# A two-layer encoder on one core: order of the first gate units of each feed-forward part pinned, and the last key projection moved by one block

## The chip, the cores and the metric

One Trainium2 chip, one core. The metric is the device time of one execution in microseconds. The engines are TensorE (PE, with its weight loads PEld), VectorE (DVE), ScalarE (ACT), GpSimd (POOL) and SyncE (SP), whose queue issues nearly all DMAs.

## The reference, cut

The input is x of 1 × 1024 × 1024 in float32. Layer 0 mixes with multi-head latent attention, layer 1 with differential attention; each layer is

```python
h = _layernorm(ALPHA * h + mix, ln_mix_g[i], ln_mix_b[i])
h = _layernorm(ALPHA * h + _swiglu(h, ffn_w_gu[i], ffn_w_down[i]), ln_ffn_g[i], ln_ffn_b[i])
```

with

```python
def _swiglu(x, w_gu, w_down):
    gate, up = jnp.split(x @ w_gu, 2, axis=-1)
    return (jax.nn.silu(gate) * up) @ w_down
```

The hidden width D_FF is 2816. In mixer B each of 8 heads has two softmax maps over 1024 keys in blocks of 128 queries (chunk-causal mask, ALiBi distances), and the output is map 0 minus lambda times map 1, times the values.

## The kernel before

**Precision.** Every large product is made of three matmuls in fp32r: a high part (a cast on ACT) and a low part (the source minus the high part, a subtract on DVE or POOL) of each operand, high × high, high × low, low × high. `split` (L501) makes the pair, and `op_unit` (L508) makes it for one unit of weights, 128 × 512, in one of a few shared buffers. So each block of weights goes DMA, cast on ACT, subtract on DVE or POOL, then PE.

**The feed-forward part** (`ffn`, L520) is a Strassen-like scheme of seven products on 2 × 2 blocks. A unit n (22 of them in a layer) is one block of w_gu, with four sub-blocks a11, a12, a21, a22; the products have the names "1", "2", "6", "7", "5", "4" and "3", 12 matmuls of 512 columns each. "1" and "2" use x itself, the others sums of blocks of x (t1, t2, t3, t4, b22), made by `raw_x` (L463) and cast by `part` (L706). `prepare` (L569) makes a product's operand: sums of sub-blocks on DVE (L579 a21 + a22, L581 a21 − a11, L583 a12 − a11, L587 a22 − a11), then `op_unit`. `consume` (L595) issues the matmuls (L547) and what reads the result. "6", "7" and "4" add into one PSUM bank, gb: after "6" DVE reads it (L629, into tmp), after "7" again (L633), and after "4" (L639). The next of the three can't begin before the read. "5" and "3" go to gc and are added by L631 and L635, "1" and "2" to ga.

**The early units.** For the first npre = 6 units "1" and "2" come first, while the last rows of the layer norm ahead are not there yet: `load_pre` (L559) loads half of unit n's block (tile gp, 2 buffers) and makes both operands, with the subtract on POOL for n = 0, 1 and on DVE from 2 on; `gates(n)` (L681) issues the products of units n and n + 1, and for n > 0 stores their results to DRAM (pg_dr), from which they are loaded again later. `load` (L553) loads a whole unit (tile gr, 1 MB).

**The layer norm** (L163) of a block of 128 rows: two means (nmu, L166, L167), squares on ACT (L170), the centred rows (L176), variance (ve, L178), a power on POOL (rs, L180), the result (L183). `raw_x` transposes it on PE (xTp), and DVE and ACT make the blocks of x (L482 to L486). In front of FFN1 the last such block, z_a, runs between the early units (`pending`).

**Mixer B.** `fill` slots say which projection is issued beside which block of attention. For head h, `proj_b` (L1369) makes queries (which = 0) and keys (which = 1), half by half: 24 matmuls, then casts (L1395) and subtracts (L1396) into the key tile bk. `score_b` (L1398) makes the scores of a block of 128 queries for both maps (L219; the maximum L222 on DVE, the exponential L227 on ACT), a reciprocal (L1411), and the difference of the maps (L1412 on POOL, L1413 on DVE); `turn_b` transposes it (pt, L148), `mix_b` multiplies it by the values. Three PSUM banks serve the scores.

**What sets the order.** The instructions are listed by a scheduler with high and low priorities from program order, so that an edit re-orders neighbours on all engines. `behind(i, j)` (L155) is a pin: instruction i may not stand ahead of j on their engine; it adds no semaphore.

## Time and profile before

| | |
|---|---|
| time, median of 3 runs | 2272.02 us (2271.24 to 2272.13) |
| the profiled execution | 2270.85 us |
| its span | 2269.1 us |
| PE busy | 2240.7 us |
| mean granted clock | 0.997 |
| FFN of layer 0 | about 440 to 1080 us |
| mixer B | about 1080 to 1545 us |
| FFN of layer 1 | about 1622 to 2269 us |

Busy times are of one profiled execution. A matmul record's start is when PE takes it; neighbours overlap, so the distance of two starts tells the rate, not the duration. A value in brackets behind a row is the idle time of that engine ahead of it, and what ended it. PEclk is the clock granted to TensorE as a share of the full one. Buffer numbers are left out of the trace's names, so gb, gr, op_g and tmp of all units read alike. The line numbers are those of the kernel before.

### The profile page before, as it was taken

The numbers are of one execution on the slowest core, as the hardware profiler recorded it, in microseconds if no ns is written. First come the engines' busy times: TensorE is split into PE (matmuls) and PEld (weight loads), VectorE is DVE, ScalarE is ACT, GpSimd is POOL, SyncE is SP. The second block draws the span as 40 slices with busy tenths as digits, with TensorE's granted clock in tenths as the row PEclk, the third lists the DMA queues.
The fourth block names the chain that finished last, engine by engine and source line by source line (L and its number), as shares of the span: only waits on it lengthen the run. The fifth ranks groups of instructions, "written<-read, shape, count | busy, mean of one in ns | idle before, by whom it ended". The sixth has DMA issues, their size and how long they took to land.

```text
span 2269.1 us, 31052 instructions
## 1 busy us (share of the span) xinstructions
PE 2240.7 (99%) x11410; PEld 1913.2 (84%) x11410; DVE 1547.0 (68%) x2894; ACT 1013.8 (45%) x2097; POOL 775.2 (34%) x626
## 2 busy tenths in 40 slices
PE   8999999999999999999999999999999999999998
PEld 8899998888888888888888898988778888888886
DVE  5676665686766667777576667576687656668778
ACT  4455564342333334445465656564432333334444
POOL 2232341114444440455432424221114444430561
PEclk9999999999999999999999999999999999999999
DMA  5010125434435338554310212053244223238443
GB/s 203 14 35 31 42 70 194 143 128 144 171 135 199 119 122 329 184 187 158 103 47 24 66 38 69 14 221 139 103 155 151 93 98 111 96 113 326 166 179 151
DMA packets 105545, 287.76 MB, mean 127 GB/s; under 512 B 7968, under 2 KB 30112, under 8 KB 94896
## 3 DMA queue, kind: packets, MB, share of 16 engines
q1 hardware_dynamic: 101552, 277.44, 34.4%
q0 software_dynamic: 3840, 8.33, 1.4%
q8 instruction: 90, 1.47, 0.3%
q14 instruction: 63, 0.52, 0.1%
HBM read 204.47 MB, written 77.07 MB: 124 GB/s over the span
## 4 chain that ended last, share of the span: by engine, by line
PE 94%; DVE 3%; DMA 1%; issue 1%; ACT 1%; POOL 0%; SPq 0%; DVEq 0%; POOLq 0%
PE gb L547 15%; PE ga L547 10%; PE gc L547 10%; PE dw L858 7%; PE dx L858 5%; PE s_a L219 4%; PE zp_a L417 3%; PE s_b L219 3%; PE dv L858 3%; PE dy L858 3%; PE bp L145 3%; PE bp L143 3%; PE bp L144 3%; PE o_a L262 2%; PE o_b L262 2%; PE hq L1107 1%
## 5 line engine op out<-in xcount | busy, mean ns | idle before, releaser
L503 ACT CAST op_g<-gr 128x512 fp32r<-128x512 f32 x240 | 146.7, 621 | 369.9 <-PE gb L547 183.1
L504 POOL TENSOR_TENSOR op_g<-gr,op_g 128x512 fp32r<-128x512 f32 x104 | 145.7, 1406 | 248.0 <-ACT op_g L503 139.6
L504 DVE TENSOR_TENSOR op_h<-rh,op_h 128x512 fp32r<-128x512 f32 x152 | 142.3, 962 | 49.4 <-ACT op_h L503 49.4
L547 PE MATMUL ga<-xh_m,op_g 128*128 128x512 f32 x512 | 168.2, 389 | 0.0
L858 PE MATMUL dw<-op_w_t,op_h 128*128 128x512 f32 x660 | 151.3, 390 | 0.0
L503 ACT CAST op_h<-rh 128x512 fp32r<-128x512 f32 x152 | 91.8, 619 | 126.7 <-PE dx L858 35.4
L858 PEld LDWEIGHTS dw<-op_w_t,op_h 128*128 128x128 f32 x660 | 123.5, 188 | 25.9 <-DVE op_h L504 0.4
L227 ACT ACTIVATE l_b<-l_b,mx_b 128x256 f32<-128x256 f32 (+7 forms) x128 | 99.4, 776 | 75.3 <-DVE mx_b L222 73.4
L504 POOL TENSOR_TENSOR op_w_b<-rw_b,op_w_b 128x512 fp32r<-128x512 f32 x44 | 64.3, 1484 | 175.5 <-ACT op_w_b L503 168.2
L858 PE MATMUL dx<-op_w_b,op_h 128*128 128x512 f32 x528 | 121.5, 390 | 1.0 <-DVE op_w_b L504 1.0
L1412 POOL TENSOR_SCALAR l_b<-l_b,rb,cst 128x128 f32<-128x128 f32 (+3 forms) x64 | 52.5, 821 | 203.8 <-DVE rb L1411 192.5
L504 DVE TENSOR_TENSOR op_g<-gr,op_g 128x512 fp32r<-128x512 f32 x136 | 110.6, 818 | 14.2 <-ACT op_g L503 14.0
L547 PE MATMUL gb<-t4h_f,op_g 128*128 128x512 f32 x352 | 115.8, 390 | 3.1 <-DVE tmp L633 3.1
L858 PEld LDWEIGHTS dx<-op_w_b,op_h 128*128 128x128 f32 x528 | 98.8, 188 | 23.0 <-DVE op_w_b L504 2.6
L547 PE MATMUL gb<-t2h_f,op_g 128*128 128x512 f32 x352 | 115.6, 390 | 0.4 <-DVE op_g L504 0.4
L547 PE MATMUL gc<-t1h_f,op_g 128*128 128x512 f32 x352 | 115.6, 389 | 0.0
L547 PE MATMUL gc<-b22h_f,op_g 128*128 128x512 f32 x352 | 115.3, 389 | 0.0
L547 PE MATMUL gb<-t3h_f,op_g 128*128 128x512 f32 x352 | 115.2, 389 | 0.0
L547 PEld LDWEIGHTS ga<-xh_m,op_g 128*128 128x128 f32 x512 | 96.1, 188 | 20.0
L504 POOL TENSOR_TENSOR op_g<-s,op_g 128x512 fp32r<-128x512 f32 x40 | 55.1, 1378 | 167.1 <-ACT op_g L503 158.8
L143 PE MATMUL bp<-xT_f,h_wb 128*128 128x512 f32 x256 | 101.6, 397 | 0.0
L144 PE MATMUL bp<-xT_f,h_wb 128*128 128x512 f32 x256 | 101.5, 397 | 0.0
(388 smaller groups left out, 6696.5 us busy)
## 6 DMA issues: line engine op xcount, KB each, us to landing
gr<-in_w_gu SPq DMA_DIRECT2D x44, 1024.0 KB, 6.9
rh<-h_dr SPq DMA_DIRECT2D x28, 1024.0 KB, 5.4
h_dr<-sh SPq DMA_DIRECT2D x22, 1024.0 KB, 5.1
h_dr<-hp SPq DMA_DIRECT2D x22, 768.0 KB, 4.1
tt<-in_w_dn SPq DMA_DIRECT2D x22, 512.0 KB, 7.3
rh<-h_dr SPq DMA_DIRECT2D x12, 768.0 KB, 4.4
wo_dr<-op_pwo SPq DMA_DIRECT2D x16, 512.0 KB, 3.5
z<-xs_dr SPq DMA_DIRECT2D x16, 512.0 KB, 11.9
```

The lines of the kernel that those rows point to most:

```text
L143: T.matmul(ps_out, lh, rh, start=(i == 0), stop=False)
L144: T.matmul(ps_out, lh, rl, start=False, stop=False)
L145: T.matmul(ps_out, ll, rh, start=False, stop=(i == n - 1))
L219: T.matmul(s[:, :w], lh, rh[:, ks], start=(j == 0), stop=(j == len(q_pass) - 1))
L227: ends["exp"] = A.activation(l[:, :n], l[:, :n], AF.Exp, bias=mx, scale=-1.0, accum_out=sm).ins
L262: T.matmul(po[:, c], a, b[:, j % 2, c], start=st, stop=sp_, skip_group_check=True)
L417: T.matmul(m, a[:, h, :], self.wo[h][w][:, c], start=(start and h == heads[0] and a is oh and w == 0), stop=(stop and h == heads[-1] and a ...
L503: turns["cast"] = A.copy(hi, src).ins
L504: return eng.tensor_tensor(lo, src, f32(hi), ALU.subtract).ins
L547: T.matmul(o, w[:, a, k * P:(k + 1) * P], x[b][:, k, :], start=(first and k == 0 and (a, b) == (0, 0)), stop=(k == 3 and a == 1), skip_gro ...
L858: T.matmul(o, h[:, a, c], w[:, b_], start=(first and (a, b_) == (0, 0)), stop=(last and a == 1), skip_group_check=True,).ins for a, b_ in ...
L1412: G.tensor_scalar(l1[:, :n], l1[:, :n], r[:, 1:2], nlam, ALU.mult, ALU.mult)
```

## The change

Three regions are touched: the start of the FFN in layer 0, its start in layer 1 (the same code), and the last head of mixer B. The number of matmuls, casts, subtracts and transfers is the same.

- `layer_norm` records its centred rows and its last result, `raw_x` its last operation, `consume` the copy of unit n's first product. In `load_pre` the subtracts of unit 2 are pinned behind the centred rows, those of units 3 to 5 behind the layer norm's result; the first cast of unit 3 is pinned behind the copy of the last first product issued.
- `load_pre(3)` is called after `gates(0)`.
- The first sum of units 0 and 1 (L579) is pinned behind raw_x's last operation.
- The products "6", "7", "4" of units 0 and 1 take turns in the program's order.
- The casts of b22 are pinned behind unit 4's last cast, those of t3 behind unit 5's first.
- In the last head of mixer B the last half of the key projection is issued in slot 4 rather than 5.

```diff
@@ layer_norm
         centred = V.scalar_tensor_tensor(y, z, nmu[:, 1:2], g, ALU.add, ALU.mult)
+        ends["centred"] = centred.ins
...
-            V.scalar_tensor_tensor(y[:, c], y[:, c], rs, b[:, c], ALU.mult, ALU.add)
+            ends["ln"] = V.scalar_tensor_tensor(y[:, c], y[:, c], rs, b[:, c], ALU.mult, ALU.add).ins
@@ raw_x
-            V.tensor_tensor(b21, b21, b12, ALU.add)
+            ends["x"] = V.tensor_tensor(b21, b21, b12, ALU.add).ins
@@ load_pre
                 ops[n, pr] = op_unit(t[:, i], eng, f"gp{layer}_{n}_{pr}")
+                early_cast[n, pr] = turns["cast"]
+                if eng is V:
+                    behind(turns["last"], ends["centred" if n == 2 else "ln"])
+                if n == 3 and pr == "1":
+                    behind(turns["cast"], ends["p1"])
@@ prepare
-                V.tensor_tensor(a21, a21, a22, ALU.add)
+                i = V.tensor_tensor(a21, a21, a22, ALU.add).ins
+                if n < 2:
+                    behind(i, ends["x"])
@@ consume
-                    A.copy(p1, acc[n, "a"])
+                    ends["p1"] = A.copy(p1, acc[n, "a"]).ins
@@ ffn
-        for n in range(4):
+        for n in range(3):
             load_pre(n, G if n < 2 else V)
         gates(0)
+        load_pre(3, V)
...
-        for n in range(NFF):
-            stream += [(n, pr) for pr in ("674" if n < 2 else "67543" if n < npre else "1627543")]
+        stream += [(n, pr) for pr in "674" for n in range(2)]
+        for n in range(2, NFF):
+            stream += [(n, pr) for pr in ("67543" if n < npre else "1627543")]
...
         load_pre(4, V)
+        cast = turns["cast"]
         for k in range(4):
             part("b22", k, r22, V)
+            behind(turns["cast"], cast)
         load_pre(5, V)
+        cast = early_cast[5, "1"]
...
             part("t3", k, r11, V)
+            behind(turns["cast"], cast)
@@ mixer B
-            for j, slot in enumerate((2, 3, 5, 6) if h < H - 1 else (1, 2, 3, 5)):
+            for j, slot in enumerate((2, 3, 5, 6) if h < H - 1 else (1, 2, 3, 4)):
```

In the rows that follow, the numbers behind a name tell buffers, and lines of the changed kernel are up to 14 higher than those of the kernel before for the same code.

On DVE in front of FFN1, in the layer norm of the last rows (nmu, z_a and ve belong to it, op_gp_2 to the early unit 2, xr_m to the blocks of x); before:

```order
L167 TENSOR_SCALAR nmu_a_1_16093<-sum_a_1_16036 128x1
L504 TENSOR_TENSOR op_gp_2_2_16160<-gp_2_16155,op_gp_2_2_16160 128x512
L504 TENSOR_TENSOR op_gp_2_1_16157<-gp_2_16155,op_gp_2_1_16157 128x512
L484 TENSOR_TENSOR xr_m_15516<-xr_m_15515,xTp_a_0_0_16106 128x4x128
L485 TENSOR_TENSOR xr_m_15514<-xr_m_15514,xTp_a_0_1_16111 128x4x128
L176 SCALAR_TENSOR_TENSOR z_a_0_15945<-z_a_0_15945,nmu_a_1_16093,gb_15518 128x1024
L178 TENSOR_SCALAR ve_a_1_16100<-ssq_a_1_16096 128x1
L486 TENSOR_TENSOR xr_m_15514<-xr_m_15514,xr_m_15517 128x4x128
L183 SCALAR_TENSOR_TENSOR z_a_0_15945<-z_a_0_15945,rs_a_1_16102,gb_15518 128x1024
```

and now:

```order
L167 TENSOR_SCALAR nmu_a_1_16093<-sum_a_1_16036 128x1
L485 TENSOR_TENSOR xr_m_15516<-xr_m_15515,xTp_a_0_0_16106 128x4x128
L486 TENSOR_TENSOR xr_m_15514<-xr_m_15514,xTp_a_0_1_16111 128x4x128
L176 SCALAR_TENSOR_TENSOR z_a_0_15945<-z_a_0_15945,nmu_a_1_16093,gb_15518 128x1024
L179 TENSOR_SCALAR ve_a_1_16100<-ssq_a_1_16096 128x1
L487 TENSOR_TENSOR xr_m_15514<-xr_m_15514,xr_m_15517 128x4x128
L505 TENSOR_TENSOR op_gp_2_1_16157<-gp_2_16155,op_gp_2_1_16157 128x512
L505 TENSOR_TENSOR op_gp_2_2_16160<-gp_2_16155,op_gp_2_2_16160 128x512
L184 SCALAR_TENSOR_TENSOR z_a_0_15945<-z_a_0_15945,rs_a_1_16102,gb_15518 128x1024
```

The two subtracts of unit 2 moved from ahead of the blocks of x to between the last of them and the layer norm's result.

On DVE in FFN1, from the read of unit 0's "6" (tmp_0 from gb_0) to the read of its "7" (gr_3 and gr_4 are the blocks of units 3 and 4); before:

```order
L629 TENSOR_TENSOR tmp_0_16519<-pg_0_16137,gb_0_16518 128x512
L504 TENSOR_TENSOR op_g_2_6_16556<-gr_2_16397,op_g_2_6_16556 128x512
L631 TENSOR_TENSOR tmp_0_16519<-tmp_0_16519,gc_05_16450 128x512
L579 TENSOR_TENSOR gr_4_16552<-gr_4_16552 128x512
L631 TENSOR_TENSOR tmp_0_16519<-tmp_0_16519,gc_03_16468 128x512
L629 TENSOR_TENSOR tmp_1_16582<-pg_0_16137,gb_1_16581 128x512
L581 TENSOR_TENSOR gr_4_16552<-gr_4_16552 128x512
L631 TENSOR_TENSOR tmp_1_16582<-tmp_1_16582,gc_15_16484 128x512
L583 TENSOR_TENSOR gr_4_16552<-gr_4_16552 128x512
L587 TENSOR_TENSOR s_1_4_16776<-gr_4_16552 128x512
L631 TENSOR_TENSOR tmp_1_16582<-tmp_1_16582,gc_13_16500 128x512
L633 TENSOR_TENSOR tmp_0_16519<-pg_0_16137,gb_0_16518 128x512
```

and now, where the row ahead of these is `gr_3`'s first sum (L585):

```order
L637 TENSOR_TENSOR tmp_0_16519<-pg_0_16137,gb_0_16518 128x512
L589 TENSOR_TENSOR gr_3_16420<-gr_3_16420 128x512
L505 TENSOR_TENSOR op_g_2_6_16559<-gr_2_16397,op_g_2_6_16559 128x512
L639 TENSOR_TENSOR tmp_0_16519<-tmp_0_16519,gc_05_16450 128x512
L595 TENSOR_TENSOR s_1_3_16681<-gr_3_16420 128x512
L591 TENSOR_TENSOR gr_3_16420<-gr_3_16420 128x512
L585 TENSOR_TENSOR gr_4_16555<-gr_4_16555 128x512
L637 TENSOR_TENSOR tmp_1_16539<-pg_0_16137,gb_1_16538 128x512
L639 TENSOR_TENSOR tmp_0_16519<-tmp_0_16519,gc_03_16466 128x512
L589 TENSOR_TENSOR gr_4_16555<-gr_4_16555 128x512
L639 TENSOR_TENSOR tmp_1_16539<-tmp_1_16539,gc_15_16484 128x512
L641 TENSOR_TENSOR tmp_0_16519<-pg_0_16137,gb_0_16518 128x512
```

Between the two reads stand ten operations as before, but unit 3's sums came in, unit 4's first sum is the sixth of them rather than the third, and its other two went behind. In layer 0 there are fifteen between the same two reads, ten before, and unit 0's "6" stands 20 matmuls sooner on PE. In both layers the store of the results of the early units 4 and 5 (pg_dr) now stands ahead of the load of unit 3's block (gr_3) in SP's queue, and two matmuls of unit 2's "5" stand ahead of unit 0's "4" on PE.

On PE in the last head, at the scores of head 7's block 6 (s_b_6) and block 7 (s_b_7), with the transposes of head 6's block 7 (pt_b_7); before:

```order
L219 MATMUL s_b_6_1_0_14903<-bk_10192,bq_10190 128x448
L219 MATMUL s_b_6_1_0_14903<-bk_10192,ql_10195 128x448
L219 MATMUL s_b_6_1_1_14908<-bk_10192,bq_10190 128x448
L219 MATMUL s_b_6_1_1_14908<-bk_10192,ql_10195 128x448
L148 MATMUL pt_b_7_0_15012<-ident,l_b_7_0_14769 128x128 x4
L219 MATMUL s_b_7_0_0_14986<-bk_10192,bq_10190 128x512
L219 MATMUL s_b_7_0_0_14986<-bk_10192,ql_10195 128x512
```

and now:

```order
L220 MATMUL s_b_6_1_0_14903<-bk_10192,bq_10190 128x448
L220 MATMUL s_b_6_1_0_14903<-bk_10192,ql_10195 128x448
L220 MATMUL s_b_6_1_1_14908<-bk_10192,bq_10190 128x448
L220 MATMUL s_b_6_1_1_14908<-bk_10192,ql_10195 128x448
L220 MATMUL s_b_7_0_0_14986<-bk_10192,bq_10190 128x512
L220 MATMUL s_b_7_0_0_14986<-bk_10192,ql_10195 128x512
L148 MATMUL pt_b_7_0_15012<-ident,l_b_7_0_14798 128x128 x4
```

Two score matmuls of the next block moved ahead of the transposes; the key projection's 24 matmuls, with its casts and subtracts, stand further ahead, before a projection of values (bv) that they followed.

More of the change, by code (lines that the diff above doesn't have):

```diff
@@ L535, in ffn @@
         npre = 6
-        r, tmp, ops, acc, hp, pg = {}, {}, {}, {}, {}, {}
+        r, tmp, ops, acc, hp, pg, early_cast = {}, {}, {}, {}, {}, {}, {}
         pg_dr = dr.tile([npre // 2, P, 4, 512], F32, name=f"pg_dr{layer}")
```

## The prediction

> **What bounds the kernel now.** I read the profile page first, then the table of PE's waits, then the stretches around the longest of them, the granted clock by windows of 3.41 us, and last the timelines of DVE, ACT and POOL at each wait. From the page:
>
> ```profile
> span 2269.1 us, 31052 instructions
> ...
> PE 2240.7 (99%) x11410; PEld 1913.2 (84%) x11410; DVE 1547.0 (68%) x2894; ACT 1013.8 (45%) x2097; POOL 775.2 (34%) x626
> ```
>
> PE is busy for 99% of the span, so an edit that removes no matmul can win only from what PE waits, 2269.1 − 2240.7 = 28.4 us, and from time that PE runs at half clock (which counts as busy). The table of PE's waits (us in total, times, longest us) names the places:
>
> ```profile
> PE hq L1107 <- ACT wih L1076: 4.6, 1, 4.6
> PE gb L547 <- DVE tmp L633: 3.1, 2, 1.7
> PE xTp_a L148 <- DVE z_a L183: 2.2, 1, 2.2
> PE s_b L219 <- DVE bk L1396: 1.3, 1, 1.3
> ...
> PE pt_b L148 <- DVE l_b L1413: 0.8, 2, 0.7
> ```
>
> The first row is the start of the program, which no edit touches. The other four lie in just the three regions that the change re-orders: 3.1 at the product "4" of unit 0 in each layer's FFN, 2.2 at the transpose behind the last layer norm ahead of FFN1, 1.3 and 0.7 in the last head of mixer B. Together 7.4 us. The windows (PE, PEld, DVE, ACT, POOL busy with counts, then the granted clock) show what two of these places cost beyond the wait:
>
> ```profile
> 494.95:498.36 3.41, 2.01 (x9) 1.36 (x8) 3.38 (x5) 0.95 (x2) 1.28 (x1) 1.00 0.00 0
> 1495.05:1498.47 3.42, 1.52 (x8) 1.09 (x8) 3.36 (x8) 0.60 (x2) 0.38 (x1) 1.00 1.02 411
> 1498.47:1501.88 3.41, 3.41 (x11) 2.58 (x10) 2.54 (x11) 2.95 (x7) 0.15 (x1) 0.50 1.03 396
> 1628.17:1631.59 3.42, 1.24 (x10) 1.06 (x10) 2.77 (x4) 2.21 (x4) 0.92 (x1) 1.00 0.42 153
> 1631.59:1635.00 3.41, 3.41 (x10) 2.63 (x9) 0.92 (x2) 3.34 (x7) 0.00 (x0) 0.50 1.04 342
> ```
>
> After a window in which PE was busy for 1.52 or 1.24 of 3.41 us, the next 3.41 us are granted 0.50 of the clock, and PE is busy in all of them: each such window costs 3.41 / 2 = 1.7 us. After 2.01 of 3.41 busy (494.95) nothing happened, so the limit lies between 1.52 and 2.01. The sum at stake is 7.4 + 2 × 1.7 = 10.8 us. The Trainium skill ("TensorE: Matmul & The Clock Gate", section "Why this matters for your kernels") puts the drop at PE-idle gaps of more than about 3 us; the rows disagree, since here 1.9 and 2.2 us of idle in a window were enough.
>
> **Base.** The profiled execution took 2270.85 us, 1.75 more than its span and 1.17 less than the median, 2272.02. The sum is made in the profiled execution and subtracted from the median. Two times of this kernel can be told apart when they differ by about 0.2%, 4.5 us.
>
> **Part 1: FFN0, unit 0's "4".** The product "4" adds into the PSUM bank gb that "6" and "7" used, so PE must wait until DVE's L633 has read the "7". FFN0's share of the wait, and DVE (and one POOL row) there:
>
> ```profile
> PE gb L547 <- DVE tmp L633: 1.4, 1, 1.4
> ```
>
> ```profile
> 488.51 0.69 DVE L629 TENSOR_TENSOR tmp<-pg,gb 128x512 f32<-128x512 f32 x1 [0.94 <-PE gb L547]
> ...
> 495.00 1.78 DVE L587 TENSOR_TENSOR s<-gr 128x512 f32<-128x512 f32 x1
> 496.70 0.67 DVE L631 TENSOR_TENSOR tmp<-tmp,gc 128x512 f32<-128x512 f32 x1
> 497.30 0.67 DVE L633 TENSOR_TENSOR tmp<-pg,gb 128x512 f32<-128x512 f32 x1
> ```
>
> ```profile
> 494.65 1.58 POOL L504 TENSOR_TENSOR op_g<-gr,op_g 128x512 fp32r<-128x512 f32 x1 [1.32 <-ACT op_g L503]
> ```
>
> DVE issues such operations 0.60 us apart (496.70 to 497.30), and takes 1.1 more for one that runs beside POOL's (1.78 against 0.67). The order after the change has 15 operations between L629 of unit 0 and its L633, not 10, but puts the product "6" that L629 waits for 20 matmuls sooner on PE. A matmul takes 0.23 us (1627.76 to 1627.99, below): 4.6 us, so L629 at 488.51 − 4.6 = 483.9. Then 16 steps of 0.60 put L633 at 493.5, at 494.6 with one operation slowed by POOL. It has to be 1.4 sooner than 497.30, that is by 495.9, for no wait: met by 1.3 to 2.4. I take the whole 1.4; the bounds are 0 and 1.4. Two matmuls of unit 2's "5" also move ahead of the "4", 0.46 of cover. What stands behind it: the load of unit 3, now behind the store of pg to DRAM in SP's queue, and DVE's L579 on that load, which stands ahead of unit 1's L629. If that load is late, PE's "7" of unit 1 is next to wait (rival C).
>
> **Part 2: last key projection one block sooner.** The rows at the scores of head 7, block 6:
>
> ```profile
> 1495.54 0.69 DVE L1396 TENSOR_TENSOR bk<-bp,bk 64x512 fp32r<-64x512 f32 x1
> ...
> 1496.61 1.28 DVE L1413 SCALAR_TENSOR_TENSOR l_b<-l_b,rb,l_b 128x1024 f32<-128x1024 f32 x1
> ```
>
> ```profile
> 1496.29 0.47 PE L219 MATMUL s_b<-bk,bq 128*128 128x448 f32 x1 [1.26 <-DVE bk L1396]
> ...
> 1498.03 0.69 PE L148 MATMUL pt_b<-ident,l_b 128*128 128x128 f32 x4 [0.66 <-DVE l_b L1413]
> ```
>
> The 24 matmuls of the projection, its two casts and two subtracts go ahead of the values of that block; the 24 are only moved. The wait of 1.26 for L1396 goes. What is late next is the softmax of head 6, block 7: L1413 ends at 1497.89 and the transpose of its result follows. L1396 no longer stands ahead of L1413 (0.6 less), but an L222 of the next scores now does (about 0.7 by its neighbours), so L1413 ends where it ended. PE comes to the transpose earlier and waits there for most of what it had waited before; it has two more score matmuls done by then, 2 × 0.23 = 0.46, and loses some 0.2 because the three score banks make it wait for L222 at two places. Gain on the path: 0.25, between 0 and 2.0 (both waits). The clock is the larger part: the idle time comes in three pieces rather than two, and the program reaches the place 1.4 us sooner against windows that run on by themselves, so less of the idle falls in one window. I take it that PE's share passes the limit of 1.52 to 2.01 and the half-clock window goes; of its 1.7 the chain of softmax results behind it takes back 0.7, as PE at full clock runs into L1413 of the next block. So 0.25 + 1.0 = 1.25, with 0.25 if the clock drops again.
>
> **Part 3: FFN1, behind the last layer norm.** The timelines of DVE, POOL, ACT and PE:
>
> ```profile
> 1623.55 2.03 DVE L504 TENSOR_TENSOR op_gp<-gp,op_gp 128x512 fp32r<-128x512 f32 x2
> 1625.49 0.67 DVE L484 TENSOR_TENSOR xr_m<-xr_m,xTp_a 128x512 f32<-128x512 f32 x1
> ...
> 1628.01 0.67 DVE L486 TENSOR_TENSOR xr_m<-xr_m,xr_m 128x512 f32<-128x512 f32 x1
> 1629.13 1.28 DVE L183 SCALAR_TENSOR_TENSOR z_a<-z_a,rs_a,gb 128x1024 f32<-128x1024 f32 x1 [0.44 <-POOL rs_a L180]
> ```
>
> ```profile
> 1621.88 2.54 POOL L504 TENSOR_TENSOR op_gp<-gp,op_gp 128x512 fp32r<-128x512 f32 x2 [6.24 <-ACT op_gp L503]
> 1628.17 0.93 POOL L180 TENSOR_TENSOR rs_a<-ve_a,cst 128x1 f32<-128x1 f32 x1 [3.75 <-DVE ve_a L178]
> ```
>
> ```profile
> 1625.08 0.18 ACT L170 ACTIVATION_READ_ACCUMULATOR zp_a<-z_a,nmu_a 128x1 f32 x1
> ```
>
> ```profile
> 1627.76 0.39 PE L547 MATMUL ga<-xl_m,op_gp 128*128 128x512 f32 x1
> 1627.99 0.39 PE L547 MATMUL ga<-xh_m,op_gp 128*128 128x512 f32 x1
> 1630.56 1.06 PE L148 MATMUL xTp_a<-ident,z_a 128*128 128x128 f32 x8 [2.18 <-DVE z_a L183]
> ```
>
> The two subtracts of unit 2 hold DVE from 1623.55 to 1625.49, 1.94 us, ahead of the layer norm's chain. Pinned behind `centred` they come after L486: L486 then starts 1.94 sooner, at 1626.07, the two take 2 × 0.60, and L183 can start at 1626.07 + 0.60 + 1.20 = 1627.87 rather than 1629.13, 1.26 sooner (POOL's power, 0.93, is hidden by the two; ACT's squares end at 1625.26, before L178 needs them). Against that, L484 now runs in the stretch to 1624.42 in which POOL is still subtracting; of the two subtracts' excess of 0.7 (2.03 against 2 × 0.67) I leave 0.3 there. So 0.95, between 0.5 and 1.26. The Trainium skill ("GPSIMD Engine Reference", section "Specifications") says that POOL shares its SBUF interfaces with VectorE and that instructions with two SBUF inputs contend; the 1.78 row above agrees. L484 reads one input from PSUM, so by that rule it is not slowed and this term would be 1.26.
>
> PE's wait falls from 2.18 to about 1.2, and PE is then busy for over 2.1 of any window of 3.41 here: above 2.01, so no half-clock window follows, 1.7 more. The lines that lose by the pins are unit 3's and 4's subtracts and loads, with L183 now queued behind two subtracts; the load of unit 4 waits for their buffer and is issued 2.4 us later (1627.87 − 1625.49). PE needs units 3 to 5 only after the 24 matmuls (24 × 0.23 = 5.5 us) of each unit between, which are the cover; if it is gone PE waits what is missing, at most those 2.4 us.
>
> **Part 4: FFN1, unit 0's "4".**
>
> ```profile
> 1674.36 0.68 DVE L629 TENSOR_TENSOR tmp<-pg,gb 128x512 f32<-128x512 f32 x1
> ...
> 1677.31 0.69 DVE L579 TENSOR_TENSOR gr<-gr 128x512 f32<-128x512 f32 x1 [1.07 <-DMA gr<-in_w_gu]
> ...
> 1680.32 1.80 DVE L583 TENSOR_TENSOR gr<-gr 128x512 f32<-128x512 f32 x1
> ...
> 1683.24 0.68 DVE L633 TENSOR_TENSOR tmp<-pg,gb 128x512 f32<-128x512 f32 x1
> ```
>
> Of the 8.9 us between L629 and L633, 1.07 is a wait for unit 4's load and 1.1 the slowing beside POOL. The number of operations between stays 10, but unit 4's L579 is the sixth of them instead of the third, when its load is there, and L583 and L587 of unit 4 move behind L633; two matmuls of unit 2's "5" move ahead of the "4" on PE (0.46). 11 steps of 0.60 are 6.6, and with one slowing 7.7: 1.2 to 2.3 sooner, and 0.46 of cover, against 1.7 to be removed. It goes. What may come is that L579 of unit 3 now stands directly ahead of L629 of unit 0 and waits for a load issued later: between 0 and 0.9 us at unit 1's "7"; I take 0.4. So 1.3.
>
> Edits with no price: the turns of units 0 and 1 (PE already takes "6" and "7" of both in turn), L579 behind the last operation of raw_x, and the casts of b22 and t3 behind other casts, which all have ACT at 45% as cover.
>
> **Sum.** 1.4 + 1.25 + 0.95 + 1.7 + 1.3 = 6.6 us; the profiled execution would take 2264.25 and the median 2272.0 − 6.6 = 2265.4.
>
> **Rivals.** A, everything goes: both waits of part 2 and the whole of its 1.7, the 2.2 of the layer norm too: 10.8, less the 0.4 of part 4, 10.4: 2261.6. For it: the places are exactly those of the table; against: L183 and L1413 are chains on DVE that the change shortens but doesn't remove. Chance 0.1.
>
> B, the waits shrink but the half-clock windows stay: in part 2 because three pieces of idle still fill one window, in part 3 because another gap nearby falls in the same window. Then 6.6 − 1.0 − 1.7 = 3.9: 2268.1, no change that can be told. For it: the windows run on by themselves, so where the gaps fall in them is luck, and the median's executions may have had fewer of them than the profiled one. Against: 2.01 of 3.41 was not enough to drop, and part 3's gap is well under that. By the 3 us of the Trainium skill (the same section) the drops would not come from these gaps at all and would stay. Chance 0.22, with the cases in which only one part of the waits goes.
>
> C, slower: the load of unit 3's weights decides. It is asked for later in both layers, and DVE's L579 on it now stands ahead of L629 of a unit whose bank PE is about to need; all of DVE stands behind it.
>
> ```profile
> gr<-in_w_gu SPq DMA_DIRECT2D x44, 1024.0 KB, 6.9
> ...
> z<-xs_dr SPq DMA_DIRECT2D x16, 512.0 KB, 11.9
> ```
>
> At 6.9 us from issue to landing it is in time, or late by the 0.4 above. To make the kernel slower by 4.5 it would have to cost PE 6.6 + 4.5 = 11.1 in two layers, 5.6 in each: a landing at some 12.5 us, as z<-xs_dr has it on a busy queue (11.9). At that the time is 2276.5. It begins to decide at 3.3 each. Against: nothing else of that size is in the queue there. Chance 0.05.
>
> D, the change moves instructions without moving PE's waits (DVE is as late with other work in the same place): 0 to 1: 2271.5. Chance 0.04, counted with no change.
>
> **How the numbers follow.** The forecast has 0.59, A 0.1, B 0.22, C 0.05, D 0.04. The forecast's own range is 2263.5 to 2267.4 (parts 2 and 3 at their bounds; its upper end is still 4.6 below). The range for 8 in 10 reaches half way to A and over B: 2262.3 to 2269.2. Faster by over 0.2%: 0.59 + 0.1 = 0.69; within: 0.22 + 0.04 = 0.26; slower: 0.05.
>
> **What would show it.** In the profile after: no wait of gb on L633 in either FFN (parts 1 and 4); xTp_a's wait on L183 near 1.2 and the clock at 1.00 behind it (part 3); no wait on L1396 and one of about 1 to 1.5 on L1413 with the clock at 1.00 behind it (part 2). A new wait of gb on L629 is part 4's 0.4; above 3 it is rival C. A clock of 0.50 at either place is rival B. The prediction is wrong if the sum of PE's waits in the three regions falls by under 2 us, or if a new wait over 2 us is there.

## The result and the profile after

The changed kernel takes 2267.42 us in the median of 13 runs, the kernel before 2272.83 in 13 runs beside it; the ratio is 0.9974, with a 95% interval of 0.9965 to 0.9983. By the ratio that is 5.9 us less, 3.9 to 8.0; the medians differ by 5.4. The forecast was 2265.4, 6.6 us less. One execution of the changed kernel (4560.46 us) and one of experiment e2 (2786.26 us, at a mean clock of 0.753) lie far outside the rest; they count in the medians and not in the ratios. The profiled execution of the changed kernel took 2268.24. From its page:

```profile
span 2266.5 us, 31066 instructions
...
PE 2240.2 (99%) x11410; PEld 1912.8 (84%) x11410; DVE 1542.9 (68%) x2894; ACT 1014.3 (45%) x2097; POOL 773.9 (34%) x626
```

PE's busy time fell by only 0.5 us, and PE's waits are in other places. The table of waits of the changed kernel (us in total, times, longest; the rows left out between these are the same in both kernels):

```profile
...
PE cp L148 <- DVE cn L1143: 1.9, 1, 1.9
PE gb L548 <- DVE tmp L637: 1.4, 1, 1.4
PE xTp_a L148 <- DVE z_a L184: 1.3, 1, 1.3
...
PE s_b L220 <- DVE mx_b L223: 0.8, 2, 0.6
...
PE pt_b L148 <- DVE l_b L1427: 0.8, 2, 0.6
PE zp_a L418 <- DMA wo<-wo_dr: 0.8, 1, 0.8
```

The wait of gb fell from 3.1 to 1.4 and is now on another line: L637 reads a "6" (L629 before), where the kernel before waited for the read of a "7". The wait on L1396 is gone; in its place two of 0.8 stand in the last head, on the maximum of the scores (L223) and on the load of the output projection's weights (wo), beside the 0.8 on the difference of the maps (L1427, L1413 before) that was there already. The first row lies in code that no edit touches (1.2 before). The granted clock by windows (PE, PEld, DVE, ACT, POOL busy, then the clock) shows a half-clock window, but not where it was:

```profile
30.19:33.60 3.41, 1.50 (x11) 1.20 (x10) 3.35 (x16) 1.26 (x5) 3.01 (x3) 1.00 0.83 239
33.60:37.02 3.42, 3.42 (x13) 3.42 (x12) 1.57 (x4) 2.00 (x5) 0.67 (x2) 0.50 0.80 296
...
1494.51:1497.92 3.41, 2.31 (x9) 1.09 (x7) 3.41 (x10) 2.00 (x7) 1.19 (x1) 1.00 1.06 301
1497.92:1501.33 3.41, 2.98 (x19) 2.50 (x19) 2.67 (x10) 2.46 (x8) 0.17 (x1) 1.00 1.02 419
1627.63:1631.04 3.41, 2.09 (x14) 1.58 (x13) 2.66 (x5) 1.10 (x2) 0.05 (x1) 1.00 0.41 80
1631.04:1634.45 3.41, 3.41 (x17) 2.80 (x16) 1.60 (x4) 1.58 (x4) 0.00 (x0) 1.00 1.02 352
```

Both windows that the prediction wanted to remove are gone. One came at 33.60 us, in code that the change doesn't touch: there the windows' position decides, which differs from execution to execution (in the kernel before the window there began at 30.74, PE was busy for 2.20 of it, and full clock followed). So two spans alone don't tell what a part is worth. I cut each profiled execution at the starts of matmuls that every version has: layer 0's unit 0 "1", layer 0's unit 8 "6", the scores of head 6's block 4, the first output projection of row block 5, layer 1's unit 0 "1", and layer 1's unit 6 "6". The stretches between, in us, with all experiments:

| kernel | start (untouched) | FFN0's start | last head | FFN1's start | median us, ratio (with interval) to runs of the kernel before made beside it |
|---|---|---|---|---|---|
| before | 441.08 | 155.81 | 95.03 | 121.31 | 2272.83 |
| changed | 442.75 | 154.10 | 95.27 | 118.50 | 2267.42, 0.9974 (0.9965 to 0.9983) |
| e1 key back | 441.87 | 154.12 | 95.60 | 118.66 | 2267.99, 0.9979 (0.9970 to 0.9988) |
| e3 unit 2 free | 443.23 | 154.11 | 95.34 | 120.04 | 2268.63, 0.9981 (0.9972 to 0.9990) |
| e4 no turns | 442.29 | 154.16 | 95.44 | 119.89 | 2269.15, 0.9985 (0.9976 to 0.9994) |
| e5 read first | 441.12 | 155.18 | 95.16 | 118.22 | 2267.40, 0.9977 (0.9968 to 0.9986) |
| e2b key alone | 441.98 | 156.09 | 95.35 | 122.18 | 2271.73, 0.9998 (0.9989 to 1.0007) |
| e7 wo first | 440.93 | 155.06 | 97.58 | 118.82 | 2269.78, 0.9985 (0.9976 to 0.9994) |
| e9 late sums | 442.06 | 154.13 | 95.34 | 118.06 | 2266.56, 0.9972 (0.9962 to 0.9982) |
| e10 no x | 441.84 | 154.16 | 95.04 | 117.70 | 2266.44, 0.9970 (0.9959 to 0.9982) |
| e11 both | 441.16 | 154.13 | 95.13 | 119.15 | 2266.73, 0.9975 (0.9965 to 0.9984) |
| e13 LN first | 441.54 | 154.16 | 95.49 | 119.25 | 2268.45, 0.9979 (0.9971 to 0.9988) |
| e14 no x, key back | 440.65 | 154.15 | 95.49 | 121.97 | 2269.79, 0.9987 (0.9978 to 0.9996) |

The changed kernel wins 1.7 us in FFN0, 2.8 in FFN1, loses 0.2 in the last head, and lost 1.7 at the untouched start by its window at half clock. 1.7 + 2.8 − 0.2 = 4.3 us from the change, against 5.4 between the medians and 5.9 by the ratio. The first column spreads over 2.6 us without any edit to it; its mean over the 13 rows is 441.7, so the profiled execution of before was 0.6 luckier than that, and of the changed kernel 1.0 unluckier. What is left of the difference, 1.1 us to the medians and 1.6 to the ratio, no trace here shows; 4.3 lies inside the interval. (The expectations below count layer 0 to unit 6, which is 38.9 us less than to unit 8.)

Each stretch is from one execution. In the last head, the eight profiles with the changed kernel's order on PE there (changed, e3, e4, e5, e9, e10, e11, e13) lie between 95.0 and 95.5, so a loss of 0.2 is no loss that can be told. In FFN1 the changed kernel, e1 and e7, in the same order on PE, lie between 118.5 and 118.8. In FFN0 the changed kernel, e1 and e9 have the same order and 154.1, but e7, with that order too, 155.06 (see there). The intervals of the ratios of all edits to the changed kernel overlap that of the changed kernel, so what is said of the experiments rests on these stretches and not on the whole times.

### The profile page after: what moved, and what is told of

The parts are those of the page before. It is cut to its first block, busy times and chain, and to the rows that moved or that the text cites. A ratio compares the mean times of both kernels' runs of the same rounds, so it can differ in the third digit from the quotient of the medians.

```text
span 2266.5 us, 31066 instructions
## 1 busy us (share of the span) xinstructions
PE 2240.2 (99%) x11410; PEld 1912.8 (84%) x11410; DVE 1542.9 (68%) x2894; ACT 1014.3 (45%) x2097; POOL 773.9 (34%) x626
## 4 chain that ended last, share of the span: by engine, by line
PE 94%; DVE 2%; DMA 1%; issue 1%; ACT 1%; POOL 0%; SPq 0%; DVEq 0%; POOLq 0%; ACTq 0%
PE gb L548 15%; PE gc L548 10%; PE ga L548 10%; PE dw L872 7%; PE dx L872 5%; PE s_a L220 4%; PE zp_a L418 3%; PE s_b L220 3%; PE dv L872 3%; PE dy L872 3%; PE bp L145 3%; PE bp L143 3%; PE bp L144 3%; PE o_a L263 2%; PE o_b L263 2%; PE hq L1121 1%
```

## The experiments

Each edit is to the changed kernel, unless it says otherwise; the diffs show the lines that differ from it.

**e1: the key projection back in its slot.**

```diff
-            for j, slot in enumerate((2, 3, 5, 6) if h < H - 1 else (1, 2, 3, 4)):
+            for j, slot in enumerate((2, 3, 5, 6) if h < H - 1 else (1, 2, 3, 5)):
```

> The changed kernel with the last key projection back in slot 5; the rest of the change stays. Theory 1, from the trace after the change: moving the projection is worth nothing on the path, because the loads of the output projection's weights (wo) start 1 to 3.5 us later and PE waits for one of them; so undoing it leaves the time within 0.8 us of the changed kernel, some 5 us faster than the kernel before. The wait of the scores on L1396 comes back (1.3 us) and the wait of zp_a on the load of wo (0.8 us) goes. Theory 2, the prediction: the projection is worth 1.25 us, and 3 us where the half-clock window comes back, so 2.4 to 4.2 us faster than before. They agree if the half-clock window is in the profile.

Measured: 0.6 us slower than the changed kernel by the medians, 0.3 in the last head. Its windows show the half clock again in the last head:

```profile
1494.02:1497.43 3.41, 1.49 (x8) 1.04 (x8) 3.35 (x7) 0.65 (x2) 0.47 (x1) 1.00 1.03 414
1497.43:1500.84 3.41, 3.41 (x12) 2.53 (x11) 2.54 (x11) 2.95 (x7) 0.05 (x1) 0.50 1.04 400
```

So 1.3 us of wait and a half-clock window of 1.7 us are back, and the stretch is 0.3 us longer. Theory 1 holds, but the wait on the load of wo is still there with 0.3 us.

**e2 and e2b: the key projection alone, on the kernel before.** The edit of the change's last line alone.

> The kernel before with the last key projection in slot 4, nothing else of the change. Theory 1: the stretch of the last head and the output projection takes 95.0 to 95.6 us from the scores of head 6's block 4 to the products of row block 5 whatever the slot (95.03 before, 95.27 after), because the softmax results and the loads of wo set it; the time stays within 0.6 us of the kernel before. Theory 2, the prediction: 1.25 us faster, with 93.8 us there.

The first run gave 2272.27 us, ratio 0.9996 (0.9987 to 1.0005), without a profile that can be compared. So it was run again:

> Once more the kernel before with only the last key projection in slot 4, for a profile at the ordinary clock; the first look was 0.8 us faster in the median than the kernel before, between what the theories gave. Theory 1: the stretch from the scores of head 6's block 4 to the products of row block 5 stays at 95.0 to 95.6 us, because loads and softmax results take the gain back. Theory 2: it falls by at least 0.8 us, to 94.2 or less.

Measured: 95.35 us in the last head, ratio 0.9998. Theory 1 holds: alone the projection brings nothing. Its table of waits has `bk` no more, and in its place

```profile
PE s_b L219 <- DVE mx_b L222: 1.0, 3, 0.6
PE zp_a L417 <- DMA wo<-wo_dr: 0.9, 1, 0.9
PE pt_b L148 <- DVE l_b L1413: 0.8, 2, 0.6
```

In FFN1, whose order on PE is the one of before, no half clock followed in this profile, and yet the stretch is 0.9 us longer: DVE waits 2.2 us for unit 4's load there (1.1 in the kernel before), and PE a new 2.0 us for the read of unit 1's "6" behind it.

**e3: unit 2's subtracts without their pin.**

```diff
-                if eng is V:
-                    behind(turns["last"], ends["centred" if n == 2 else "ln"])
+                if eng is V and n > 2:
+                    behind(turns["last"], ends["ln"])
```

> The changed kernel without the pin of unit 2's two subtracts; those of units 3 to 5 stay pinned. Theory 1: the two subtracts go back ahead of the layer norm's chain, PE's wait on L183 in front of FFN1 grows from 1.3 to about 2.2 us, and where PE is then busy for less than about 1.5 us of a window of 3.41 the clock drops to half behind it: 0.9 us plus 1.7 us slower than the changed kernel, 2.6 in all, or 3 us faster than the kernel before. Theory 2: the half-clock window is not caused by that gap, and the loss is the 0.9 us of the wait alone.

Measured: FFN1's start 1.5 us longer. PE's wait on the layer norm is 2.1 us, and the windows there show the clock:

```profile
1628.05:1631.46 3.41, 1.32 (x8) 0.82 (x7) 2.59 (x4) 1.51 (x3) 0.93 (x1) 1.00 0.44 163
1631.46:1634.87 3.41, 3.41 (x14) 2.93 (x12) 2.84 (x5) 2.21 (x5) 0.00 (x0) 0.50 0.95 300
```

Theory 1 on the cause: the gap brings the half clock. The loss is less than 2.6, since the wait of gb in FFN1 fell from 1.4 to 0.6 at the same time: 0.8 + 1.7 − 0.8 = 1.7 against 1.5 measured.

**e4: units 0 and 1 without turns.**

```diff
-        stream += [(n, pr) for pr in "674" for n in range(2)]
-        for n in range(2, NFF):
-            stream += [(n, pr) for pr in ("67543" if n < npre else "1627543")]
+        for n in range(NFF):
+            stream += [(n, pr) for pr in ("674" if n < 2 else "67543" if n < npre else "1627543")]
```

> The changed kernel with the program order of units 0 and 1 as before (6, 7, 4 of unit 0, then those of unit 1). Theory 1: the 1.5 us gained in layer 0 come from the turns, which put two products between a unit's 7 and its 4 and bring the read of 7 early enough; without them a wait of gb on the read of unit 0's 7 or 6 of 1 to 2.5 us is back in at least one layer, and the time is 1.5 to 3 us longer than the changed kernel. Theory 2, the prediction's step that gave the turns no price: no wait of gb over 0.3 us more than in the changed kernel, time within 0.5 us of it.

Measured: FFN0 unchanged, FFN1 1.4 us longer, with two waits of gb in FFN1 in place of the one:

```profile
PE gb L548 <- ACT tmp L665: 1.3, 1, 1.3
PE gb L548 <- DVE tmp L641: 1.2, 1, 1.2
```

So the turns do have a price, 1.4 us, as theory 1 said, but not the one it gave: layer 0's gain doesn't come from them. (e3 and e10 leave FFN0 at 154.1 too. So none of these three edits carries layer 0's 1.7 us alone; the pins of units 3 to 5, the later call of `load_pre(3)` and the pins of the casts were not taken back singly, and which edit carries it stays open.)

**e5: the read of unit 1's "6" ahead of unit 3's second sum.**

```diff
-                V.tensor_tensor(u2, p1, acc[n, "b"], ALU.add)
+                ends["read6", n] = V.tensor_tensor(u2, p1, acc[n, "b"], ALU.add).ins
...
-                V.tensor_tensor(a11, a21, a11, ALU.subtract)
+                i = V.tensor_tensor(a11, a21, a11, ALU.subtract).ins
+                if n == 3:
+                    behind(i, ends["read6", 1])
```

> The changed kernel with one more pin: unit 3's second sum, and what follows from it, behind the read of unit 1's 6 (L629 of the kernel before). Theory 1: the wait of 1.4 us that is left in FFN1 is that read standing in DVE's queue behind unit 3's sums, one of which ran beside POOL at 1.78 us; with the pin the read is about 1.7 us earlier, the wait is 0 to 0.3 us and the time 1.1 to 1.4 us shorter than the changed kernel. Theory 2: the wait is due to the load of unit 3, whose first sum still stands ahead of the read; then at least 1 us of the wait stays and the time stays within 0.5 us.

Measured: neither. The wait at unit 1's "7" in FFN1 is gone, but two others came there (0.5 and 0.2 us in the table of waits), and the stretch gained 0.3, no more than profiles of one order differ there. In FFN0, where there had been no wait, one of 0.8 on the read of unit 0's "7" appeared, and FFN0 lost 1.1: the read of unit 1's "6", for which DVE waits 1.3 us, now stands ahead of unit 3's and unit 4's sums, and the read of unit 0's "7" behind them.

**e7: the loads of z behind the output projection's weights.**

```diff
-            nc.sync.dma_start(self.z[tb], self.x_src[tb * P:(tb + 1) * P, :])
+            if not first:
+                nc.sync.dma_start(self.z[tb], self.x_src[tb * P:(tb + 1) * P, :])
...
                     self.wo.append([x.bitcast(F32R) for x in t])
+            for tb in LAST_ORDER[:2]:
+                nc.sync.dma_start(self.z[tb], self.x_src[tb * P:(tb + 1) * P, :])
```

> The changed kernel with the two loads of z_a, which wait in the queue ahead of the output projection's weights, issued behind those weights; the scheduler also puts one product of wo_0 earlier. Theory 1, a chain: the wait of zp_a on the load of wo (0.8 us) goes, but the next transpose (pt_b of head 7, block 7) waits for its softmax results that much longer, and the stretch of the last head stays at 95.0 to 95.5 us, the time within 0.4 us of the changed kernel. Theory 2: the load is what took back the key projection's gain, and with it out of the way the stretch falls by 0.8 us or more, to 94.5.

Measured: 2.3 us longer in the last head; both theories failed. The scheduler put the first product of wo_0 ahead of products of the values, where PE still waits 0.9 us for the load, and the transposes of the last blocks wait 2.2 us. As the order of PE changed too, the run doesn't tell what the loads alone cost.

Its FFN0 took 155.06, though the order of layer 0 is that of the changed kernel: DVE waited 1.21 us for unit 3's load (gr), and PE 0.7 for a cast at unit 1's "7". So 1 us of layer 0's 1.7 can be lost again to a load that lands later.

**e9: in layer 1, the sums of units 3 and 4 behind the read of unit 1's "6".**

```diff
-                V.tensor_tensor(u2, p1, acc[n, "b"], ALU.add)
+                ends["read6", n] = V.tensor_tensor(u2, p1, acc[n, "b"], ALU.add).ins
...
                     behind(i, ends["x"])
+                elif layer == 1 and n in (3, 4):
+                    behind(i, ends["read6", 1])
```

> The changed kernel with, in layer 1 alone, the first sums of units 3 and 4 (and so all that follow from them) behind the read of unit 1's 6. Theory 1: the 1.4 us wait of gb in FFN1 is that read standing behind those sums in DVE's queue; it now comes 1.7 to 3 us earlier, the wait goes, FFN1's start (from its first product to unit 6's) falls from 118.5 to 117.1 us and the time by 1.4 us. Theory 2: DVE has too much to do in this stretch, whatever its order, and the wait only moves to the next product that waits for DVE; FFN1's start falls by 0.3 us at most, as with the pin on unit 3's second sum alone.

Measured: 0.4 us less in FFN1's start, near theory 2. The wait of 1.4 at unit 1's "7" is gone; PE waits at unit 1's "4" instead:

```profile
1685.33 0.50 PE L548 MATMUL gb<-t4h_f,op_g 128*128 128x512 f32 x1 [0.50 <-DVE tmp L643]
```

**e10: without the pin behind raw_x's last operation.**

```diff
-                if n < 2:
-                    behind(i, ends["x"])
```

> The changed kernel without the pin of the first sums of units 0 and 1 behind raw_x's last operation. In the order this alone puts layer 0's unit 0 6 back 16 matmuls later, where it was before the change. Theory 1: this pin, to which the prediction gave no price, carries layer 0's gain: a wait of gb on unit 0's read of 7 of 0.8 to 1.5 us is back in layer 0, FFN0's start takes 116.0 to 116.9 us in place of 115.2, and the time is about 1.5 us longer than the changed kernel. Theory 2: the gain comes from DVE's order between the two reads; then nothing of the wait comes back, 115.2 us.

Measured: FFN0 keeps its gain (theory 2), and FFN1's start is 0.8 us shorter. In FFN0 the read of unit 0's "6" is again as late as in the kernel before, but DVE gets from it to the read of the "7" faster (e10's lines are 6 above before's here):

```profile
489.27 0.69 DVE L635 TENSOR_TENSOR tmp<-pg,gb 128x512 f32<-128x512 f32 x1 [1.37 <-PE gb L548]
490.49 0.69 DVE L585 TENSOR_TENSOR gr<-gr 128x512 f32<-128x512 f32 x1 [0.53 <-DMA gr<-in_w_gu]
...
496.51 0.68 DVE L639 TENSOR_TENSOR tmp<-pg,gb 128x512 f32<-128x512 f32 x1
```

7.2 us, where the kernel before took 8.8 (488.51 to 497.30) for as many operations. A wait for a load still stands between them, 0.53 us for unit 3's here and 0.63 for unit 4's before; what is gone are the two operations slowed beside POOL, 1.78 and 0.95 us in the kernel before, where all of e10's take 0.69 or less.

**e11: e9 and e10 together.**

> The changed kernel without the pin behind raw_x's last operation, and with the first sums of units 3 and 4 of layer 1 behind the read of unit 1's 6. Without the pin alone FFN1's start took 117.7 us with 0.6 us of gb's wait left; with the late sums alone 118.1, where the wait had moved to unit 1's 4. Theory 1: DVE has too much work in this stretch, and the two together give no more than the better of them, 117.5 to 118.1 us. Theory 2: the two waits are of different origin and add up: 117.0 us, 0.7 us faster than without the pin alone.

Measured: 119.15, longer than either. PE's wait at "4" is 0.5 as in e9, and a new one of 0.8 us on ACT's copy of an early unit's product appears ahead of it. That is 0.6 more than the changed kernel's, too. Neither theory; the gains don't add.

**e13: on e10, unit 2's second subtract behind the layer norm in layer 1.**

```diff
-                    behind(turns["last"], ends["centred" if n == 2 else "ln"])
+                    behind(turns["last"], ends["centred" if (n, pr) == (2, "1") or layer == 0 and n == 2 else "ln"])
```

> The changed kernel without the pin behind raw_x's last operation, and in layer 1 with unit 2's second subtract behind the layer norm's result. Theory 1: POOL's power is done 0.1 us after the first subtract, so L183 starts 0.5 to 0.6 us sooner, PE's wait on it falls from 1.4 to 0.8 us, and FFN1's start from 117.7 to 117.1 us. Theory 2: PE's next wait takes it back, as unit 2's second product now comes later: FFN1's start within 0.2 us of 117.7.

Measured: the wait fell to 0.8 as theory 1 said, but the stretch grew to 119.25, which neither theory has, since the load of unit 4 is now issued behind the store of the layer norm's rows; its subtract, for which DVE waits 4.29 us (on the cast of that load), stands ahead of L485 in DVE's queue, and PE waits for that:

```profile
PE gb L548 <- DVE tmp L635: 1.2, 1, 1.2
PE ga L548 <- DVE xr_m L485: 1.1, 1, 1.1
PE xTp_a L148 <- DVE z_a L184: 0.8, 1, 0.8
```

**e14: on e10, the key projection back in its slot.**

> The changed kernel without the pin behind raw_x's last operation and with the last key projection back in slot 5. Theory 1: the projection's slot is worth at most 0.5 us: the stretch of the last head takes 95.0 to 95.6 us, with a half-clock window there or without one. Theory 2, the prediction: 1.25 us more than without the pin alone, 96.3 us.

Measured: 95.49 in the last head, theory 1, and this time with no half-clock window there. The waits on L1396 and on the loads of wo both stand in its table:

```profile
PE s_b L220 <- DVE bk L1408: 1.3, 1, 1.3
PE zp_a L418 <- DMA wo<-wo_dr: 1.0, 1, 1.0
PE pt_b L148 <- DVE l_b L1425: 0.8, 2, 0.7
```

What nobody expected is FFN1's start, 121.97. Moving the projection ripples into FFN1's order, and without the pin the scheduler put the first sum of unit 0 ahead of the blocks of x. DVE waits there for the load, PE for DVE, and the clock halves behind it (DVE, PE, then the windows):

```profile
1635.11 0.69 DVE L585 TENSOR_TENSOR gr<-gr 128x512 f32<-128x512 f32 x1 [4.93 <-DMA gr<-in_w_gu]
```

```profile
1637.15 0.77 PE L548 MATMUL ga<-xh_m,op_gp 128*128 128x512 f32 x1 [2.36 <-DVE xr_m L485]
```

```profile
1633.54:1636.95 3.41, 1.24 (x6) 0.70 (x4) 1.84 (x4) 3.38 (x6) 0.00 (x0) 1.00 1.03 429
1636.95:1640.37 3.42, 3.22 (x8) 2.58 (x9) 3.42 (x7) 3.42 (x8) 0.00 (x0) 0.50 0.17 67
```

This is what the pin behind raw_x's last operation is for. With the projection in slot 5 its lack costs 121.97 − 118.66 = 3.3 us (e14 against e1); with slot 4, in e10, the order happens to be good without it and the stretch is 0.8 shorter. Without the pin, moving the projection shifts FFN1's start by 121.97 − 117.70 = 4.3 us; with it, by 0.2 (e1 against the changed kernel). None of the versions beats the changed kernel by more than the intervals; e10 has the lowest median, 2266.44, of 6 runs.

## Why the prediction was right, and where it was wrong

The size came out near, 5.9 for 6.6, and two of four parts were right; the others erred by −1.5 and −1.0, and layer 0 was 0.3 better than forecast. The parts add up to 4.3 us, so that the whole came nearer to the forecast than its parts is luck as far as the traces go. By the prediction's own sign it was a close thing: the waits in the three regions fell from 7.4 to 5.3 us, by 2.1, and under 2 was to mean wrong.

**Part 1 (1.4 forecast, 1.7 measured): right, though not all of its argument was needed.** The wait of 1.4 is gone; the other 0.3 I can't place. The changed kernel's rows, DVE at L629's and L633's successors (L637, L641):

```profile
485.65 0.69 DVE L637 TENSOR_TENSOR tmp<-pg,gb 128x512 f32<-128x512 f32 x1 [1.00 <-PE gb L548]
...
494.03 1.46 DVE L585 TENSOR_TENSOR gr<-gr 128x512 f32<-128x512 f32 x1
...
496.61 0.67 DVE L641 TENSOR_TENSOR tmp<-pg,gb 128x512 f32<-128x512 f32 x1
```

This profile reached FFN0 1.67 us later than that of before (442.75 against 441.08), so 1.67 has to be taken off to compare. L637 then stands at 483.98, where I had 483.9, and L641 at 494.94, where I had 493.5 to 494.6 with one operation slowed (here 1.46 us at 494.03); no wait needed 495.9, so about 1 us of the margin is left. e10 shows that the 20 matmuls by which "6" moved ahead weren't needed: there the read of "6" is as late as before and the gain is the same, because no operation between the two reads is slowed. Which of the edits makes either order is open (see e4).

**Part 2 (1.25 forecast, −0.2 measured): wrong.** The step that failed is "of its 1.7 the chain of softmax results behind it takes back 0.7", and with it the gain of 0.25 on the path: everything was taken back. The window went, the wait of 1.26 went, and nothing was gained. PE in the changed kernel:

```profile
1495.64 0.47 PE L220 MATMUL s_b<-bk,bq 128*128 128x448 f32 x1 [0.23 <-DVE mx_b L223]
...
1496.91 0.50 PE L220 MATMUL s_b<-bk,bq 128*128 128x512 f32 x1 [0.59 <-DVE mx_b L223]
...
1498.20 1.06 PE L148 MATMUL pt_b<-ident,l_b 128*128 128x128 f32 x8 [0.56 <-DVE l_b L1427]
...
1501.17 0.39 PE L263 MATMUL o_b<-pth_b,bvh 128*128 128x256 f32 x1 [0.15 <-ACT pth_b L251]
...
1505.50 0.73 PE L418 MATMUL zp_a<-wo,oh_a 128*128 128x512 f32 x2 [0.77 <-DMA wo<-wo_dr]
```

The first three are the waits that I had named (the one on L1427 smaller, 0.56 for 1 to 1.5); the last two weren't in the sum. Counted from the scores of block 4, the six loads of the output projection's weights are issued 1.3 us (the first) to 3.6 us (the last) later than before, and they take their turn in a busy queue; that the values behind the projection hold their buffers longer is the likely reason, not a tested one. The table says more than this one mechanism does: in twelve of the thirteen profiles the last head takes 95.0 to 95.6 us, with the projection in either slot, with the half clock (before, e1, e4) and without it. Two pairs have the same order on PE there and differ in the window: e4 with the half clock took 95.44 and the changed kernel without it 95.27; e1 with it took 95.60 and e14 without it 95.49. In each pair PE was idle for 0.9 us less where the clock was halved (1.75 against 2.69, 2.45 against 3.33). So the window that was to be worth 1.7 was worth 0.1 to 0.2, less than these profiles can tell: PE's waits and its slow window there weren't costs that could be taken away one at a time, and what is saved in one place is waited for in the next. That the loads of wo are the last to do so was argued, and e7 didn't settle it. Whether the window goes was near chance as well: with the projection in the new slot e4 still has it, and in the old slot e14 does not.

**Part 3 (0.95 and 1.7 forecast): right in both sizes, by a limit that doesn't hold.** DVE and PE in the changed kernel:

```profile
1623.84 0.69 DVE L485 TENSOR_TENSOR xr_m<-xr_m,xTp_a 128x512 f32<-128x512 f32 x1 [0.24 <-ACT xr_m L484]
...
1628.39 1.27 DVE L184 SCALAR_TENSOR_TENSOR z_a<-z_a,rs_a,gb 128x1024 f32<-128x1024 f32 x1
```

```profile
1629.72 0.55 PE L148 MATMUL xTp_a<-ident,z_a 128*128 128x128 f32 x3 [1.32 <-DVE z_a L184]
```

The wait fell by 0.86, from 2.18 to 1.32, and the clock stayed at 1.00 behind it; e3 brought both back with a wait of 2.1. By the Trainium skill ("TensorE: Matmul & The Clock Gate", section "Why this matters for your kernels"), gaps under about 3 us would leave the clock alone; e3 disagrees, as the kernel before did. I had argued the clock from PE's share alone, "over 2.1" and so above 2.01; it is 2.09 in the changed kernel, and the last section shows that PE's share alone decides nothing. The reason why the gain stayed below 1.26 was another than I gave. L184 starts 0.74 sooner (1628.39 for 1629.13), not 1.26, since L485 (L484 before), though not slowed beside POOL, 0.69 us, waits 0.24 for ACT's copy, and the centred rows (L176) come another 0.2 later behind it. That L485 isn't slowed agrees with the Trainium skill ("GPSIMD Engine Reference", section "Specifications"): it has one SBUF input.

**Part 4 (1.3 forecast, 0.3 measured): wrong in one term.** 2.8 us in FFN1, less 0.86 and 1.7, leaves 0.3 (2.81 − 2.56), and the waits say the same: 1.7 at unit 0's "4" is gone, 1.37 at unit 1's "7" came. The way to the "4" was costed right: 7.7 us from L637 at 1672.34 to unit 0's L641 at 1680.04, for 6.6 to 7.7 forecast. The term that failed is the new wait, for which I took 0.4, between 0 and 0.9:

```profile
1671.73 0.69 DVE L585 TENSOR_TENSOR gr<-gr 128x512 f32<-128x512 f32 x1 [1.41 <-DMA gr<-in_w_gu]
1672.34 0.68 DVE L637 TENSOR_TENSOR tmp<-pg,gb 128x512 f32<-128x512 f32 x1
...
1675.34 1.78 DVE L591 TENSOR_TENSOR gr<-gr 128x512 f32<-128x512 f32 x1
1677.04 0.68 DVE L585 TENSOR_TENSOR gr<-gr 128x512 f32<-128x512 f32 x1
1677.64 0.67 DVE L637 TENSOR_TENSOR tmp<-pg,gb 128x512 f32<-128x512 f32 x1
```

```profile
1678.46 0.47 PE L548 MATMUL gb<-t3h_f,op_g 128*128 128x512 f32 x1 [1.37 <-DVE tmp L637]
```

The place was right, the cause was only half. Unit 3's sum waits 1.41 us for its load and then takes 0.6 ahead of unit 0's read; besides, six operations, one of them slowed to 1.78 beside POOL, stand between that read and unit 1's. I had costed every operation on the way to unit 0's "4", and on the way to unit 1's "7", which PE reaches first, only the load. e5, e9 and e11 show that moving the reads ahead moves the wait and wins 0.4 us at most: DVE runs there from 1671.73 to 1687.9 without a gap.

Of FFN1's stretch as a whole, parts 3 and 4 together, the edits to the feed-forward part win 2.65 us with the projection in slot 5 (e1 against before) and 3.7 with slot 4 (the changed kernel against e2b).

**The edits with no price** were wrong in two of three: e4 gives the turns 1.4 us in FFN1, and e14 against e1 gives the pin behind raw_x's last operation 3.3 us (e10 0.8 the other way, where the order is good without it). The third, the pins of the casts, no run took back. I had named ACT as their cover, and the queue at stake was DVE's. **Rival C**, the load of unit 3, showed as the 1.41 us that DVE waited, far from the 3.3 from which it would decide. **Rival B**, that the half clock stays, was wrong for FFN1 and didn't matter in the last head. **Rivals A and D**, 10.4 us and at most 1, lie outside the measured interval of 3.9 to 8.0.

## What to carry to other kernels

Cost a re-ordering at every product that waits for the engine whose queue is changed, in the order in which PE reaches them, and not only at the one where the wait stood. A wait, or a stretch at half clock, is worth its length only if nothing behind it is due at a fixed time: before counting it, ask which load or chain would be late next. And with gains of a microsecond, cut two traces at the same instructions; the spans differ by more than that through code that wasn't touched.

## What the runs showed of the hardware that I had not expected

The half-clock windows come on a grid of 3.41 us (the two of the kernel before begin 133.12 us apart, 39 windows) that lies differently in each execution, and PE's busy time alone doesn't tell when one follows. Three windows (PE busy, then PEld busy), of e4, e10 and e2b:

```profile
1494.63:1498.04 3.41, 2.03 (x9) 0.86 (x8) 3.41 (x11) 1.67 (x4) 1.19 (x1) 1.00 1.02 304
1498.04:1501.46 3.42, 3.42 (x14) 3.03 (x14) 2.24 (x8) 2.10 (x6) 0.02 (x1) 0.50 1.03 422
```

```profile
1494.00:1497.42 3.42, 2.07 (x8) 0.86 (x6) 3.42 (x10) 1.88 (x5) 1.20 (x1) 1.00 1.03 317
1497.42:1500.83 3.41, 3.20 (x19) 2.53 (x19) 2.67 (x9) 2.41 (x6) 0.40 (x1) 1.00 1.03 422
```

```profile
1630.55:1633.96 3.41, 1.86 (x13) 1.70 (x14) 3.06 (x4) 2.39 (x6) 0.17 (x1) 1.00 0.42 154
```

Half clock follows the first, with 2.03 us of PE, and not the second, with 2.07, nor the third, with 1.86, which is followed by full clock as well. The limit that I read from before, between 1.52 and 2.01 of PE alone, is therefore no limit. The sum of the two columns is 2.89 in the first; it is 2.7 or less in the other windows of this document with half clock behind them, 2.93 in the second, and 3.3 or more in the others without. It also fits every other window of that grid in the thirteen traces, from 15 to 2250 us: of eight with half clock behind them none has a sum above 2.89, and of the others none is below 2.93. It is a fit with a thin margin, and no edit tested it.

An operation on DVE with both inputs in SBUF that ran beside one of POOL took 1.46 to 1.80 us in these rows in place of 0.68, in whichever position the new order put it. Reads of PSUM are spared. In the changed kernel's trace, such operations of 128 × 512 that read gb, gc or a transpose (xTp) from PSUM took 0.69 us at most with POOL at work beside them (101 of them); those with both inputs in SBUF took 0.70 at most while POOL was idle (508), and 1.76 in the median where POOL was at work for 0.6 us or more of their time (183).
